# The low halves of eleven weight blocks by an adding transfer: a two-layer decoder trunk in split float32 on one core

## Chip, core and metric

The kernel runs on one core of a Trainium2 chip. The metric is the device time of one execution in microseconds (us); lower is better. Engines are called TensorE (PE, the matrix engine), VectorE (DVE), ScalarE (ACT), GpSimd (POOL) and SyncE (SP, which issues most transfers). L412 is line 412 of the kernel before. Lines of the changed kernel are higher, by 1 from line 46 on and by 7 behind `convert`: L750 is L757 there.

## What is computed

A trunk of two layers on 512 tokens of width 1024. Each layer has one input projection whose columns feed three mixers side by side (RWKV-7, retention and latent attention), an output projection, and a gated feed-forward part. The reference, cut to its frame:

```python
for l in range(DEPTH):                       # DEPTH = 2
    hn = rms_norm(h, attn_norm[l])
    proj = hn @ w_in[l]                      # 512 x 1024 @ 1024 x 2592
    p_a, p_b, p_c = split(proj)              # RWKV 896, retention 1024, latent attention 672 columns
    y_a, v_first = rwkv7_mixer(p_a, ...)     # layer 2 mixes v with layer 1's v_first
    y_b = retention_mixer(p_b, positions)
    y_c = mla_mixer(p_c, positions, ...)     # q and kv latents -> w_q_up, w_kv_up -> causal softmax
    h = h + concat(y_a, y_b, y_c) @ w_out[l]
    hn = rms_norm(h, ffn_norm[l])
    gu = hn @ w_gate_up[l]                   # D_FF = 2816
    h = h + (silu(gu[..., :D_FF]) * gu[..., D_FF:]) @ w_down[l]
return rms_norm(h, final_norm)
```

## The kernel before

**Split products.** Activations lie transposed in SBUF, features on the partitions and the 512 tokens along them. Each float32 operand of the large products is held as two halves of the type float32r: `hi`, the rounded value, and `lo`, what the rounding left. `gemm` makes a product of three matmuls for each piece of 128 rows: hi with hi, hi with lo, lo with hi, 512 columns each (a "group" in what follows). A block of eight such pieces, [8, 128], has 1024 columns in SBUF.

**The weight stream.** All weights pass through in one fixed sequence of blocks, 102 in the first layer, so that layer 2 begins with block 102. SyncE loads a block to one of three buffers `wr` (`fetch`, L395, 512 KB for 1024 columns). `convert` (L405 to L413) makes its halves in two rings of three buffers: ScalarE copies `wr` to `wh`, which rounds it (L411), and then VectorE, or GpSimd for the blocks listed in `POOL_LO`, subtracts: `wl = wr - wh` (L412). `wnext` asks for conversions so that three blocks are ready, and `gemm` reads `wh` twice before it reads `wl`. In layer 2, blocks 113 to 115 are the retention values with the rotary key (`VGROUPS`: 864, 864 and 576 columns; their matmuls have 288 columns), 116 and 117 the retention gate, 118 and 119 the latents of keys and values, 120 to 122 those of the queries, 123 and 124 `w_kv_up`, 125 to 127 `w_q_up` (768 columns each), and 128 the first of `w_out`.

**Order.** The program is written by generators that a `Driver` interleaves: `dense` gives the large products, and `rwkv`, `chain`, `group_norm`, `retnet`, `head` and others give the small steps of the mixers in between. A step yields a due time from the table `T`, in thousands of cycles of the driver's own clock, which counts the matmuls issued so far; the generator with the best priority whose time has come goes on. The table `EN` names the engine of a small operation by a key (`d` VectorE, `p` GpSimd, `a` ScalarE). Each engine then runs its instructions in the order in which they were written, apart from moves that the framework's scheduler makes by its own estimates.

**The steps near the change, in layer 2.** In `rwkv` the value residual is made by a difference, a product (L690, key e564) and a sum (L691, e565); L711 to L715 are exponentials on ScalarE, whose results VectorE multiplies at L720 to L724; L730 and the halves behind it make two more operands; at L746 TensorE makes 16 products of 64x128 for each PSUM pair, and VectorE copies them out under a mask (L750), two copies for each pair. `pm` has four PSUM buffers, so the third pair of products waits for the first copies. In between, `dense` writes the retention queries and keys: VectorE scales a product (L1150), four transfers exchange rows of it (L1152), and L1153 to L1155 rotate it. Later, L821 and L829 move pieces of a triangular inverse from PSUM, `retnet` squares a product (L952) and multiplies with the gate (L959), `group_norm` ends with L887 to L893 (L348 and L349 belong to its inverse root), and `head` makes the softmax: scores in a PSUM buffer of `pd`, a maximum (L984), an exponential (L986).

```python
act.copy(hi[:, z], t[:, z])                                                    # L411
(pool if on in POOL_LO else dve).tensor_tensor(lo[:, z], t[:, z], hi[:, z].bitcast(F32), ALU.subtract)
...
E("e564").tensor_tensor(s, s, vf[:, b, :], ALU.mult)                           # L690
E("e565").tensor_tensor(v_[:, b, :], v_[:, b, :], s, ALU.add)                  # L691
...
dve.tensor_tensor(o, pg[par].rearrange("p (j w t) -> p j w t", j=4, w=2), m, ALU.mult)   # L750
...
dve.tensor_tensor(t, ps, rB, ALU.mult)                                         # L1150
```

Of the kernel before, what the change touches and what calls it, by code (L numbers as in the profile page):

```python
# [15 lines left out]
AF = mybir.ActivationFunctionType  # L16
ALU = mybir.AluOpType
# [115 lines left out]
def lay_out(inp):  # L133
# [57 lines left out]
def tile_trunk(ctx: ExitStack, tc: tile.TileContext, a: dict, out: bass.AP, dbg=None):  # L191
    nc = tc.nc
    act, dve, pool, sp = nc.scalar, nc.vector, nc.gpsimd, nc.sync
# [17 lines left out]
    def E(key):  # L211
        return {"d": Dve, "p": pool, "a": Act}[EN[key]]

    def times(key, o, x, f):

        if EN[key] == "a":
            act.activation(o, x, AF.Identity, scale=f)
        else:
            {"d": dve, "p": pool}[EN[key]].tensor_scalar(o, x, f, None, ALU.mult)

    def nm(s):
        uid[0] += 1
        return f"{s}_{uid[0]}"
# [6 lines left out]
    def r2(shape=(P, S), dt=F32):  # L230
        return mp.tile(list(shape), dt, tag="r2", name=nm("r2"), bufs=NR)
# [4 lines left out]
    def sm(shape, dt=F32, tag="sm", bufs=4):  # L236
        return mp.tile(list(shape), dt, tag=tag, name=nm(tag), bufs=bufs)
# [167 lines left out]
    def convert(at=0):  # L405

        t, i, j, parts, on = raw(at)
        hi, lo = (wp.tile([P, i * j], F32R, tag=n, name=nm(n)) for n in ("wh", "wl"))
        for part in range(parts):
            z = slice(part * i * j // parts, (part + 1) * i * j // parts)  # L410
            act.copy(hi[:, z], t[:, z])  # L411
            (pool if on in POOL_LO else dve).tensor_tensor(lo[:, z], t[:, z], hi[:, z].bitcast(F32), ALU.subtract)  # L412
        stream["ready"].append((1.0, tuple(z.rearrange("p (i j) -> p i j", i=i) for z in (hi, lo))))  # L413

    def load_next(parts=1):
        plan.pop(0)
        fetch(parts)
        convert()
# [14 lines left out]
    def sums(last, down, end, start):  # L433
# [30 lines left out]
        if down and not start:  # L464
            yield convert()
# [67 lines left out]
    def tables():  # L533
        yield T[0]["tables1"]
        posi = r2((P, S), I32)
# [8 lines left out]
        def angles(inv, tok=False):  # L544
# [962 lines left out]
```

## Time and profile before

| | us |
|---|---|
| median of 3 runs | 1308.99 |
| lowest and highest run | 1302.78, 1310.22 |
| the profiled execution | 1300.39 |
| its span in the trace | 1298.6 |

The mean granted clock of TensorE over the span is 0.993 of full speed. The page gives the busy time of each engine, and queries of the trace give the same for any stretch, the waits of an engine with what ended each, and single instructions in order of time. A busy time counts an engine's instructions, not what they wait for; the idle time in brackets behind an instruction is followed by what released it.

### The profile page before, as it was taken

To read this page: it belongs to the slowest core of one execution; us is meant where nothing else is said; L and a number is where in the kernel's file an instruction comes from. 1 tells how busy PE (TensorE), PEld (TensorE's weight loads), DVE (VectorE), ACT (ScalarE), POOL (GpSimd) and SP (SyncE) were. 2 spreads that over 40 slices of the span, in tenths; PEclk is the share of its full clock that TensorE was granted. 3 is DMA by queue.
4 is the path that set the end of the run, shared out by engine and by line. 5 is a ranking of instruction groups with operands and counts; after the bars stand their busy time and mean duration, and the time that the engine had idled before them with its cause. 6 is when DMAs were issued, how large, how long until landed. Compare 5 with 4: busy or idle time off the path is not lost.

```text
span 1298.6 us, 20237 instructions
## 1 busy us (share of the span) xinstructions
PE 1266.0 (97%) x7802; PEld 1089.0 (84%) x7802; DVE 988.0 (76%) x1647; ACT 683.3 (53%) x1273; POOL 114.8 (9%) x101
## 2 busy tenths in 40 slices
PE   7999999999999999999999999989999999999997
PEld 5788788678899999999877887856888999999996
DVE  7797876857987777777668697686679877777774
ACT  7834456835554444445475345465455544444454
POOL 1040112301000000000012300132100000000000
PEclk9999999999999999999999999989999999999999
DMA  7435423123233333333522523140322333222231
GB/s 250 138 92 158 102 70 110 33 66 98 82 114 98 101 111 98 101 95 106 186 91 85 135 85 78 49 164 1 98 97 74 108 113 98 97 98 98 82 114 65
DMA packets 67512, 131.14 MB, mean 101 GB/s; under 512 B 29044, under 2 KB 33940, under 8 KB 67416
## 3 DMA queue, kind: packets, MB, share of 16 engines
q1 hardware_dynamic: 66040, 128.23, 31.7%
q8 instruction: 61, 1.00, 0.3%
q10 hardware_dynamic: 1232, 1.09, 0.3%
q0 software_dynamic: 144, 0.52, 0.1%
q14 instruction: 35, 0.29, 0.1%
HBM read 117.50 MB, written 9.18 MB: 98 GB/s over the span
## 4 chain that ended last, share of the span: by engine, by line
PE 89%; DVE 5%; ACT 3%; DMA 1%; issue 1%; SPq 0%; DVEq 0%; ACTq 0%
PE pd L251 61%; PE pm L251 26%; PE pm L258 2%; DMA wr<-in_wts_dram 1%; DVE wl L412 0%; DVE r L730 0%; DVE r L1469 0%; DMA u<-in_xT_dram 0%; DVE wl L430 0%; DVE u L724 0%; DVE u L1025 0%; DVE u L720 0%; DVE u L1246 0%; ACT wh L411 0%; DVE r L440 0%
## 5 line engine op out<-in xcount | busy, mean ns | idle before, releaser
L251 PE MATMUL pd<-u,wh 128*128 128x256 f32 (+1 forms) x3136 | 757.9, 334 | 9.7 <-ACT wh L411 5.9
L251 PEld LDWEIGHTS pd<-u,wh 128*128 128x128 f32 x3136 | 530.1, 191 | 70.6 <-issue 7.3
L251 PE MATMUL pd<-u,wl 128*128 128x256 f32 (+1 forms) x1568 | 519.7, 331 | 0.2
L251 PEld LDWEIGHTS pd<-u,wl 128*128 128x128 f32 x1568 | 299.4, 191 | 28.6 <-POOL wl L412 0.8
L251 PE MATMUL pm<-u,wh 128*128 128x512 f32 (+1 forms) x800 | 211.9, 352 | 0.0
L411 ACT CAST wh<-wr 128x1024 fp32r<-128x1024 f32 (+3 forms) x102 | 98.8, 974 | 146.3 <-PE pd L251 86.3
L251 PEld LDWEIGHTS pm<-u,wh 128*128 128x128 f32 x800 | 139.1, 190 | 17.9
L251 PE MATMUL pm<-u,wl 128*128 128x512 f32 (+1 forms) x400 | 140.5, 351 | 0.0
L429 ACT CAST wh<-r 128x512 fp32r<-128x512 f32 x144 | 87.4, 618 | 98.6 <-PE pm L251 51.7
L412 DVE TENSOR_TENSOR wl<-wr,wh 128x1024 fp32r<-128x1024 f32 (+4 forms) x86 | 99.1, 1156 | 42.6 <-ACT wh L411 42.4
L429 ACT CAST wh<-wr 128x512 fp32r<-128x512 f32 x108 | 66.9, 620 | 79.5 <-PE pm L251 54.1
L430 DVE TENSOR_TENSOR wl<-r,wh 128x512 fp32r<-128x512 f32 x144 | 97.6, 687 | 8.1 <-ACT wh L429 6.0
L430 DVE TENSOR_TENSOR wl<-wr,wh 128x512 fp32r<-128x512 f32 x108 | 74.3, 689 | 24.1 <-ACT wh L429 21.8
L251 PEld LDWEIGHTS pm<-u,wl 128*128 128x128 f32 x400 | 75.8, 190 | 10.2
L412 POOL TENSOR_TENSOR wl<-wr,wh 128x1024 fp32r<-128x1024 f32 (+4 forms) x16 | 34.8, 2176 | 504.1 <-ACT wh L411 504.1
L1392 DVE TENSOR_TENSOR u<-u,pm 128x512 f32<-128x512 f32 x64 | 43.6, 684 | 43.7 <-PE pm L251 43.7
L251 PE MATMUL pm<-u,u 32*32 32x32 f32 (+4 forms) x728 | 67.4, 277 | 3.8 <-DVE u L750 2.8
L251 PEld LDWEIGHTS pm<-u,u 32*32 32x32 f32 (+3 forms) x728 | 50.5, 157 | 20.7 <-issue 13.6
L411 ACT CAST wh<-gg 128x1024 fp32r<-128x1024 f32 x32 | 33.6, 1049 | 41.7 <-issue 27.7
L440 DVE TENSOR_TENSOR r<-r,wr 128x512 f32<-128x512 f32 x72 | 49.5, 687 | 0.6
L251 PE MATMUL pd<-u,u 96*128 96x512 f32 (+3 forms) x128 | 45.2, 467 | 4.3 <-ACT u L986 3.6
L412 DVE TENSOR_TENSOR wl<-gg,wh 128x1024 fp32r<-128x1024 f32 x32 | 39.1, 1222 | 7.8 <-ACT wh L411 7.8
(272 smaller groups left out, 1593.8 us busy)
## 6 DMA issues: line engine op xcount, KB each, us to landing
wr<-in_wts_dram SPq DMA_DIRECT2D x142, 512.0 KB, 3.5
gg<-in_wts_dram SPq DMA_DIRECT2D x32, 512.0 KB, 3.3
wr<-in_wts_dram SPq DMA_DIRECT2D x22, 384.0 KB, 3.0
u<-in_xT_dram SPq DMA_DIRECT2D x7, 512.0 KB, 6.8
tb<-tab_d SPq DMA_DIRECT2D x8, 256.0 KB, 4.7
r<-r SPq DMA_DIRECT2D x32, 64.0 KB, 2.0
h_d<-u SPq DMA_DIRECT2D x4, 512.0 KB, 2.9
u<-h_d SPq DMA_DIRECT2D x4, 512.0 KB, 7.4
```

The source lines that it names most:

```text
L251: tc.keep_in_program_order(nc.tensor.matmul(o, lhsT, rhs, start=start, stop=stop, skip_group_check=True))
L258: tc.keep_in_program_order(nc.tensor.transpose(o, x, idn))
L411: act.copy(hi[:, z], t[:, z])
L412: (pool if on in POOL_LO else dve).tensor_tensor(lo[:, z], t[:, z], hi[:, z].bitcast(F32), ALU.subtract)
L429: act.copy(hi[:, z], t)
L430: dve.tensor_tensor(lo[:, z], t, hi[:, z].bitcast(F32), ALU.subtract)
L440: E(key).tensor_tensor(o, x, y, ALU.add)
L1392: dve.tensor_tensor(hk(m), hk(m), ps, ALU.add)
```

## The change

For the eleven blocks in the new list `DMA_LO` the conversion is written differently: ScalarE writes the negated rounded weights to `wl`; GpSimd issues a transfer that reads the same weights from DRAM again and adds them onto `wl`; ScalarE makes `wh` as before. VectorE or GpSimd (block 115) subtracts nothing there. `POOL_LO` changes too: in layer 1 blocks 23 and 27 go from GpSimd to VectorE, and 8 and 31 the other way; in layer 2 block 115 becomes a transfer, 129 and 134 go to VectorE, 117, 130 and 140 to GpSimd. In `EN` the product e564 (L690) goes from GpSimd to VectorE and the sum e565 (L691) from VectorE to GpSimd. In `T` 21 due times of layer 1 and 11 of layer 2 are other numbers.

```diff
-POOL_LO = (0, 12, 21, 23, 26, 27, 30, 35, 38, 106, 110, 115, 129, 134, 137)
+DMA_LO = (113, 114, 115, 118, 119, 120, 121, 122, 125, 126, 127)
+POOL_LO = (0, 8, 12, 21, 26, 30, 31, 35, 38, 106, 110, 117, 130, 137, 140)
...
-        stream["raw"].append((t, i, j, parts, stream["next"] - 1))
+        stream["raw"].append((t, src, i, j, parts, stream["next"] - 1))
...
-        t, i, j, parts, on = raw(at)
+        t, src, i, j, parts, on = raw(at)
...
             z = slice(part * i * j // parts, (part + 1) * i * j // parts)
+            if on in DMA_LO:
+
+                act.activation(lo[:, z], t[:, z], AF.Identity, scale=-1.0)
+                pool.dma_start(lo[:, z], src[:, z], accum_op=ALU.add)
+                act.copy(hi[:, z], t[:, z])
+                continue
             act.copy(hi[:, z], t[:, z])
```

The orders of the engines before and after the change follow for three places. In a row, `u`, `r` and `tb` are tiles in SBUF, `pd` and `pm` tiles in PSUM, and the last number of a name counts the tiles.

**VectorE at the masked copies of layer 2 (place A).** Before:

```order
L730 SCALAR_TENSOR_TENSOR r_1331_7122<-u_6882,PC,u_6657 128x512
L412 TENSOR_TENSOR wl_7148<-wr_7145,wh_7147 128x864
L730 SCALAR_TENSOR_TENSOR r_1332_7123<-u_6882,PC,u_6657 128x512
L1150 TENSOR_TENSOR r_1337_7134<-pd_7043,rB_6622 128x512
L1150 TENSOR_TENSOR r_1351_7205<-pd_7144,rB_6622 128x512
L750 TENSOR_TENSOR u_7172<-pm_7176,C 128x8x64
L750 TENSOR_TENSOR u_7172<-pm_7177,C 128x8x64
```

and in the changed kernel:

```order
L737 SCALAR_TENSOR_TENSOR r_1331_7117<-u_6882,PC,u_6657 128x512
L737 SCALAR_TENSOR_TENSOR r_1332_7118<-u_6882,PC,u_6657 128x512
L1157 TENSOR_TENSOR r_1337_7135<-pd_7052,rB_6622 128x512
L757 TENSOR_TENSOR u_7168<-pm_7172,C 128x8x64
L757 TENSOR_TENSOR u_7168<-pm_7173,C 128x8x64
L757 TENSOR_TENSOR u_7169<-pm_7188,C 128x8x64
L757 TENSOR_TENSOR u_7169<-pm_7189,C 128x8x64
L757 TENSOR_TENSOR u_7170<-pm_7204,C 128x8x64
L757 TENSOR_TENSOR u_7170<-pm_7205,C 128x8x64
L1161 TENSOR_TENSOR r_1338_7136<-r_1338_7136,tb_6923 128x512
L1157 TENSOR_TENSOR r_1355_7233<-pd_7145,rB_6622 128x512
```

The subtraction of block 114 between the two L730 (now L737) is gone, as is that of block 113 further up, and the second L1150 (now L1157) stands behind six of the masked copies. On TensorE, `dense`'s groups between the products that feed the copies are now two of 128x512, taken from ahead of the products, where one of 128x512 and one of 128x288 stood: ahead of the third pair of products one group of each kind fewer is issued.

**GpSimd at the same place.** Before:

```order
L725 TENSOR_TENSOR dsc_7019<-r_1310_7020,emid_7018 128x7
L725 TENSOR_TENSOR dsc_7019<-r_1324_7080,emid_7018 128x7
L315 TENSOR_TENSOR r_1334_7126<-r_1331_7122,r_1333_7125 128x512
L315 TENSOR_TENSOR r_1336_7131<-r_1332_7123,r_1335_7130 128x512
L412 TENSOR_TENSOR wl_7224<-wr_7221,wh_7223 128x576
L1153 TENSOR_TENSOR u_7042<-r_1337_7134,tb_6922 128x512
L1153 TENSOR_TENSOR u_7042<-r_1351_7205,tb_6922 128x512
```

and in the changed kernel:

```order
L732 TENSOR_TENSOR dsc_7013<-r_1310_7014,emid_7012 128x7
L415 DMA wl_7056<-in_wts_dram 128x864
L732 TENSOR_TENSOR dsc_7013<-r_1324_7075,emid_7012 128x7
L415 DMA wl_7149<-in_wts_dram 128x864
L316 TENSOR_TENSOR r_1334_7121<-r_1331_7117,r_1333_7120 128x512
L316 TENSOR_TENSOR r_1336_7126<-r_1332_7118,r_1335_7125 128x512
L1160 TENSOR_TENSOR u_7051<-r_1337_7135,tb_6922 128x512
L415 DMA wl_7252<-in_wts_dram 128x576
L1160 TENSOR_TENSOR u_7051<-r_1355_7233,tb_6922 128x512
```

The three transfers of blocks 113 to 115 stand between small operations, and the subtraction of block 115 is gone.

**ScalarE at the first softmax of layer 2 (place C).** Before:

```order
L347 ACTIVATE r_1582_8452<-r_1581_8451 128x512
L888 ACTIVATE r_1571_8414<-r_1571_8414,PC 128x512
L888 ACTIVATE r_1580_8449<-r_1580_8449,PC 128x512
L986 ACT_TABLE_LOAD
L986 ACTIVATE u_8475,ssum_8481<-pd_8477,nmx_8480 128x512
```

and in the changed kernel:

```order
L348 ACTIVATE r_1582_8466<-r_1581_8465 128x512
L895 ACTIVATE r_1571_8428<-r_1571_8428,PC 128x512
L993 ACT_TABLE_LOAD
L993 ACTIVATE u_8486,ssum_8492<-pd_8488,nmx_8491 128x512
L895 ACTIVATE r_1580_8463<-r_1580_8463,PC 128x512
```

The first exponential goes ahead of the second head group's scaling (L888, now L895). On VectorE the first maximum (L984) goes ahead of the second L887 and L889 in the same way. Place B is on ScalarE 60 us earlier, where the copy of the retention output to its rounded half (L305, called from L961) moves from ahead of the two L821 to behind the next square (L951, L952).

## Rows read from the trace of the kernel before

**Rows 1.** The page, part 1: busy us (share of the span) xinstructions of each engine.

```profile
PE 1266.0 (97%) x7802; PEld 1089.0 (84%) x7802; DVE 988.0 (76%) x1647; ACT 683.3 (53%) x1273; POOL 114.8 (9%) x101
```

**Rows 2.** Stretches: length, busy us of PE, PEld, DVE, ACT, POOL; granted clock, DMA share, GB/s.

```profile
17.00:350.00 333.00, 328.27 (x1878) 264.29 (x1879) 261.73 (x484) 193.16 (x365) 57.54 (x46) 0.99 0.33 99
690.00:1000.00 310.00, 298.81 (x1745) 240.37 (x1744) 236.50 (x439) 159.36 (x315) 46.82 (x42) 0.98 0.29 85
155.00:160.00 5.00, 3.29 (x59) 2.56 (x60) 3.42 (x6) 2.99 (x5) 0.00 (x0) 1.00 1.05 221
720.00:730.00 10.00, 8.74 (x64) 7.77 (x65) 9.86 (x14) 1.62 (x3) 9.25 (x11) 0.83 0.46 121
855.00:865.00 10.00, 9.66 (x28) 5.63 (x29) 6.88 (x24) 6.11 (x21) 4.91 (x5) 0.66 0.73 255
```

**Rows 3.** Waits of TensorE from 690 to 1010 us: us, times, longest.

```profile
PE pd L251 <- ACT u L986: 3.6, 1, 3.6
PE pm L251 <- DVE u L750: 2.5, 1, 2.5
PE pm L251 <- ACT r L952: 1.2, 1, 1.2
PE pm L251 <- ACT u L821: 0.8, 2, 0.4
```

**Rows 4.** VectorE's instructions around place A: start us, us, line, operation, [idle before].

```profile
697.38 2.30 DVE L412 TENSOR_TENSOR wl<-wr,wh 128x1024 fp32r<-128x1024 f32 x1
701.30 0.69 DVE L691 TENSOR_TENSOR u<-u,r 128x512 f32<-128x512 f32 x1 [1.62 <-POOL r L690]
...
716.43 1.05 DVE L412 TENSOR_TENSOR wl<-wr,wh 128x864 fp32r<-128x864 f32 x1
717.40 1.78 DVE L730 SCALAR_TENSOR_TENSOR r<-u,PC,u 128x512 f32<-128x512 f32 x1
719.10 1.27 DVE L1150 TENSOR_TENSOR r<-pd,rB 128x512 f32<-128x512 f32 x2
720.30 0.67 DVE L750 TENSOR_TENSOR u<-pm,C 128x512 f32<-128x512 f32 x1
```

**Rows 5.** SyncE's transfers of L1152 at place A.

```profile
696.85 2.46 SPq L1152 DMA_DIRECT2D r<-r  x4
```

**Rows 6.** ScalarE at place B.

```profile
791.30 0.62 ACT L305 CAST u<-r 128x512 fp32r<-128x512 f32 x1 [2.32 <-DVE r L959]
```

**Rows 7.** ScalarE at place C.

```profile
852.38 0.81 ACT L888 ACTIVATE r<-r,PC 128x512 f32<-128x512 f32 x1 [0.51 <-DVE r L887]
```

**Rows 8.** ScalarE's casts of blocks 119, 121 and 127, and TensorE where block 127 starts.

```profile
748.11 1.05 ACT L411 CAST wh<-wr 128x1024 fp32r<-128x1024 f32 x1 [1.95 <-PE pd L251]
...
759.75 1.06 ACT L411 CAST wh<-wr 128x1024 fp32r<-128x1024 f32 x1 [4.10 <-PE pd L251]
...
833.30 0.83 ACT L411 CAST wh<-wr 128x768 fp32r<-128x768 f32 x1 [0.87 <-PE pd L251]
...
843.50 0.62 PE L251 MATMUL pd<-u,wh 128*128 128x512 f32 x2
...
844.19 0.62 PE L251 MATMUL pd<-u,wh 128*128 128x512 f32 x2
```

**Rows 9.** GpSimd's one issue before, and transfers by kind: KB each, us to landing.

```profile
47.29 0.75 POOL L673 DMA_DIRECT2D vf_d<-u  x1 [2.00 <-DVE u L1133]
...
wr<-in_wts_dram SPq DMA_DIRECT2D x142, 512.0 KB, 3.5
wr<-in_wts_dram SPq DMA_DIRECT2D x22, 384.0 KB, 3.0
r<-r SPq DMA_DIRECT2D x32, 64.0 KB, 2.0
u<-h_d SPq DMA_DIRECT2D x4, 512.0 KB, 7.4
vf_d<-u POOLq DMA_DIRECT2D x1, 512.0 KB, 4.2
```

More of the change, by code (lines that the diff above doesn't have):

```diff
@@ L36 @@
 TWO_PI = 2.0 * math.pi
-T = [{'tables1': 0, 'norm1': 0.0, 'p_rwkv': 3.43, 'p_ret': 0, 'p_head': 6.66, 'p_tab': 2.02, 'p_gn': 0.0, 'p_att': 6.0, 'p_kr': 0.0, 'angles1': 0, 'angles2': 3.74, 'angles3': 0.0, 'angles4': 0.46, 'angles5': 3.39, 'rwkv1': 4.34, 'rwkv2': 8.45, 'rwkv3': 0, 'rwkv4': 0.0, 'rwkv5': 0, 'rwkv6': 1.03, 'rwkv7': 0.0, 'rwkv8': 2.74, 'rwkv9': 5.5, 'rwkv10': 3.21, 'rwkv11': 0.76, 'rwkv12': 4.16, 'rwkv13': 2.42, 'rwkv14': 0, 'rwkv15': 0.82, 'rwkv16': 0.36, 'rwkv17': 0.74, 'rwkv18': 14.33, 'rwkv19': 2.06, 'rwkv20': 0, 'rwkv21': 1.12, 'chain1': 0.9, 'chain2': 2.38, 'chain3': 0.55, 'group_norm1': 5.69, 'group_norm2': 3.14, 'group_norm3': 4.58, 'retnet1': 5.58, 'retnet2': 0, 'retnet3': 0.74, 'retnet4': 4.98, 'retnet5': 3.23, 'retnet6': 0, 'head1': 9.39, 'head2': 0.36, 'head3': 4.91, 'head4': 1.99, 'attend1': 1.77, 'key_rope1': 3.62, 'latent_norm1': 6.26, 'latent_norm2': 3.54, 'latent_norm3': 0.33, 'sums1': 2.61, 'sums2': 2.56, 'sums3': 0, 'sums4': 10.27, 'sums5': 3.42, 'sums6': 6.78, 'sums7': 2.65},
-     {'norm1': 0, 'p_rwkv': 5.43, 'p_ret': 7.16, 'p_head': 0, 'p_gn': 2.8, 'p_att': 0, 'p_kr': 5.54, 'rwkv1': 3.33, 'rwkv2': 5.03, 'rwkv3': 0, 'rwkv4': 0, 'rwkv5': 0, 'rwkv6': 3.29, 'rwkv7': 0, 'rwkv8': 7.7, 'rwkv9': 1.93, 'rwkv10': 2.94, 'rwkv11': 0.81, 'rwkv12': 3.89, 'rwkv13': 0.02, 'rwkv14': 0, 'rwkv15': 0.58, 'rwkv16': 0, 'rwkv17': 0.73, 'rwkv18': 13.88, 'rwkv19': 0.0, 'rwkv20': 0.42, 'rwkv21': 0.0, 'chain1': 0.28, 'chain2': 0.96, 'chain3': 0.69, 'group_norm1': 4.53, 'group_norm2': 2.33, 'group_norm3': 19.85, 'retnet1': 2.13, 'retnet2': 4.32, 'retnet3': 0, 'retnet4': 1.4, 'retnet5': 0.0, 'retnet6': 0, 'head1': 5.26, 'head2': 0.0, 'head3': 8.59, 'head4': 0.13, 'attend1': 0.0, 'key_rope1': 1.56, 'latent_norm1': 3.38, 'latent_norm2': 1.41, 'latent_norm3': 0.52, 'sums1': 2.53, 'sums2': 8.37, 'sums3': 7.02, 'sums4': 0.16, 'sums5': 4.5, 'sums6': 5.56, 'sums7': 1.81}]
@@ L41 @@
-EN = {'e499': 'd', 'e535': 'd', 'e541': 'd', 'e542': 'd', 'e563': 'd', 'e564': 'p', 'e565': 'd', 'e592': 'd', 'e593': 'd', 'e594': 'd', 'e595': 'd', 'e757': 'd', 'e759': 'p', 'e773': 'p', 'e826': 'd', 'e968': 'p', 'e969': 'd', 'e970': 'd', 'e909': 'd', 'e1037': 'd', 'e1090': 'd', 'e1096': 'p', 'e1097': 'd', 'e1171': 'd', 'e302': 'd', 'e273': 'd', 'c511': 'a', 'c639': 'a', 'c646': 'a', 'c647': 'a', 'c686': 'a', 'c716': 'a', 'c736': 'a', 'c1008': 'a', 'c498': 'd', 'h1': 'p', 'h2': 'd', 'h3': 'p', 'h4': 'p', 'h5': 'd', 'h6': 'd', 's1': 'd', 's2': 'd', 's3': 'd', 's4': 'd', 'z': 'd', 'x0': 'p', 'x1': 'd', 'x2': 'p', 'x3': 'd'}
+T = [{'tables1': 0, 'norm1': 0.0, 'p_rwkv': 3.43, 'p_ret': 0, 'p_head': 7.87, 'p_tab': 0.0, 'p_gn': 0.0, 'p_att': 5.3, 'p_kr': 0.04, 'angles1': 0, 'angles2': 3.74, 'angles3': 0.0, 'angles4': 5.7, 'angles5': 0, 'rwkv1': 4.34, 'rwkv2': 8.45, 'rwkv3': 0, 'rwkv4': 0, 'rwkv5': 0, 'rwkv6': 1.03, 'rwkv7': 0.0, 'rwkv8': 3.93, 'rwkv9': 2.08, 'rwkv10': 0, 'rwkv11': 0.76, 'rwkv12': 4.16, 'rwkv13': 2.42, 'rwkv14': 0, 'rwkv15': 0.82, 'rwkv16': 0.24, 'rwkv17': 0.74, 'rwkv18': 14.33, 'rwkv19': 2.06, 'rwkv20': 0, 'rwkv21': 0, 'chain1': 0.94, 'chain2': 2.38, 'chain3': 0.55, 'group_norm1': 5.69, 'group_norm2': 3.14, 'group_norm3': 4.75, 'retnet1': 5.58, 'retnet2': 0, 'retnet3': 1.21, 'retnet4': 4.98, 'retnet5': 3.23, 'retnet6': 0, 'head1': 9.39, 'head2': 0.36, 'head3': 4.91, 'head4': 1.99, 'attend1': 1.77, 'key_rope1': 3.62, 'latent_norm1': 6.26, 'latent_norm2': 1.2, 'latent_norm3': 0.33, 'sums1': 0, 'sums2': 0, 'sums3': 0.99, 'sums4': 14.85, 'sums5': 5.48, 'sums6': 4.38, 'sums7': 2.65},
+     {'norm1': 0, 'p_rwkv': 5.43, 'p_ret': 7.94, 'p_head': 0, 'p_gn': 2.8, 'p_att': 0, 'p_kr': 4.9, 'rwkv1': 3.33, 'rwkv2': 4.39, 'rwkv3': 0, 'rwkv4': 0.0, 'rwkv5': 0, 'rwkv6': 3.29, 'rwkv7': 0, 'rwkv8': 7.7, 'rwkv9': 1.45, 'rwkv10': 2.94, 'rwkv11': 0.81, 'rwkv12': 4.08, 'rwkv13': 0.02, 'rwkv14': 0, 'rwkv15': 0.58, 'rwkv16': 0, 'rwkv17': 0.73, 'rwkv18': 13.88, 'rwkv19': 0.0, 'rwkv20': 0.42, 'rwkv21': 0.0, 'chain1': 0.28, 'chain2': 0.96, 'chain3': 0.69, 'group_norm1': 5.32, 'group_norm2': 2.33, 'group_norm3': 15.83, 'retnet1': 2.13, 'retnet2': 4.32, 'retnet3': 0.0, 'retnet4': 1.4, 'retnet5': 0.0, 'retnet6': 0, 'head1': 5.26, 'head2': 0.0, 'head3': 8.59, 'head4': 0.09, 'attend1': 0.0, 'key_rope1': 1.56, 'latent_norm1': 3.38, 'latent_norm2': 1.41, 'latent_norm3': 0.52, 'sums1': 1.71, 'sums2': 8.37, 'sums3': 7.02, 'sums4': 0.16, 'sums5': 3.51, 'sums6': 5.56, 'sums7': 3.62}]
@@ new lines @@
+EN = {'e499': 'd', 'e535': 'd', 'e541': 'd', 'e542': 'd', 'e563': 'd', 'e564': 'd', 'e565': 'p', 'e592': 'd', 'e593': 'd', 'e594': 'd', 'e595': 'd', 'e757': 'd', 'e759': 'p', 'e773': 'p', 'e826': 'd', 'e968': 'p', 'e969': 'd', 'e970': 'd', 'e909': 'd', 'e1037': 'd', 'e1090': 'd', 'e1096': 'p', 'e1097': 'd', 'e1171': 'd', 'e302': 'd', 'e273': 'd', 'c511': 'a', 'c639': 'a', 'c646': 'a', 'c647': 'a', 'c686': 'a', 'c716': 'a', 'c736': 'a', 'c1008': 'a', 'c498': 'd', 'h1': 'p', 'h2': 'd', 'h3': 'p', 'h4': 'p', 'h5': 'd', 'h6': 'd', 's1': 'd', 's2': 'd', 's3': 'd', 's4': 'd', 'z': 'd', 'x0': 'p', 'x1': 'd', 'x2': 'p', 'x3': 'd'}
```

## Prediction

> **What bounds the kernel now.** The page first: TensorE is busy for 97% of the span, VectorE for 76% [rows 1]. The reader should take from this that time can be won only where TensorE pauses or runs at its lower clock; an instruction less on VectorE is worth nothing by itself. The table by stretches comes next [rows 2]. From 690 to 1000 us, the mixing part of layer 2, where all eleven blocks lie, TensorE is busy 298.81 of 310 us, so 11.2 us are open there. The waits of TensorE in that stretch name the pauses [rows 3]: 3.6 us for the softmax (L986), 2.5 us for VectorE's masked copies (L750), 1.2 us for a squared half (L952), 0.8 us for two copies of the triangular inverse (L821). Two of them cost more than their length, because the granted clock falls behind them to the lower of its two levels for a while. In the 10 us around and behind the L750 pause it is 0.83 on the mean, behind the softmax pause 0.66 [rows 2]. Against the full clock these lose 0.17 x 10 = 1.7 us and 0.34 x 10 = 3.4 us. After the pause of 5.00 - 3.29 = 1.71 us in layer 1 the clock stays at 1.00 [rows 2]. Pauses and clock make up everything that layer 2's half of this change can win: about 16 us.
>
> **The pause for L750 (place A).** VectorE is the late one: it goes without a gap from L1150 to L750 and the first L750 starts at 720.30 us [rows 4]. Ahead of that the change removes two subtractions of 864 columns; the shown one holds the engine from 716.43 to 717.40, 0.97 us, and the other is taken at the same. Its place on the other side is covered: the cast of that block no longer stands ahead of ScalarE's exponentials, so VectorE's next operation, which waits for them, can come as much earlier. One of the two L1150 is now issued behind the L750s: half of the step from 719.10 to 720.30, 0.60 us. The swap of the product and the sum (L690, L691) takes away VectorE's wait of 1.62 us for GpSimd. Of this only 0.6 us count, since the operation behind it (L1154, which follows when L691 ends at 702.0) needs transfers that land around 701.3: issued from 696.85 to 699.3 [rows 5], 2.0 us of landing [rows 9]. Sum: 0.97 + 0.97 + 0.60 + 0.60 = 3.1 us. Against it, one group of three 128x512 matmuls and one of three 128x288 fewer stand on TensorE ahead of the product that waits for the first L750. A group of 512 takes 844.19 - 843.50 = 0.69 us [rows 8], one of 288 by its columns 0.39, so TensorE asks 1.1 us earlier. A pause of 2.5 + 1.1 - 3.1 = 0.5 us stays, below the 1.71 us that left the clock alone. Gain: 2.0 us, and the 1.7 us of clock: **3.7 us**. Bounds: 0, if the transfer or a contended row of VectorE eats the margin, and 4.2, if the pause goes whole.
>
> **The small pauses (place B).** ScalarE's cast at 791.30 us stands, waiting for VectorE, ahead of the two L821 copies [rows 6]; it moves behind the next square. The 0.8 us for L821 go; the copies for L829 then find that cast of 0.62 us ahead of them, and I give back 0.3. The 1.2 us for L952 are the latency of ScalarE's own square and stay. Gain: **0.5 us**, bounds 0 and 1.5.
>
> **The softmax pause (place C).** TensorE waits 3.6 us for the first exponential to free a PSUM buffer [rows 3]; this stands behind the second L888 at 852.38 us [rows 7]. In the new order the first maximum (L984) and exponential go ahead of the second head group's L887, L889 and L888. That takes two operations of 0.60 us each (the step of L1150, of the same size) out of VectorE's path, and out of ScalarE's 0.8 us and the wait of 0.5 before it [rows 7]. Against it, the subtraction of block 129, on GpSimd before, now lies on VectorE ahead of L348 (1.05 x 1024/864 = 1.24 us by the row of 864 columns [rows 4]). By the two queues together I get the exponential 1.2 us earlier: **1.2 us**. The pause of 2.4 us that is left is nearer to the 2.5 us at A, which the clock followed, than to 1.71 us, so I leave the 3.4 us as they are. Bounds: 0, and 3.6 + 3.4 = 7.0 us. [...]
>
> **What is added, and what covers it.** ScalarE writes eleven negated copies: five at 1.05 and three at 0.83 us by the casts of the same shapes [rows 8], 864 columns twice at 0.89 and 576 at 0.59 by the columns; together 10.1 us on an engine that is busy 159 of 310 us there [rows 2]; the cover is TensorE's other two blocks in the ring. GpSimd issues eleven transfers. The only one it issues before takes 0.75 us and lands in 4.2 us with 512 KB; a plain load of 512 KB lands in 3.5, one of 384 KB in 3.0 us [rows 9]. The trace has no adding transfer, so it is bounded: 4.2 us if the second reading is hidden; 7.4 + 4.2 = 11.6 us if it pays the slowest load of 512 KB and a whole pass more. I take 4.2 us and the data time of a further 512 KB, 4 x (3.5 - 3.0) = 2.0 us: **6.2 us** (384 KB: 5.2), because the same queue's row is the nearest.
> Against that the room: block 119's cast starts at 748.11 us, when its buffer comes free, and the block is wanted when block 118 ends, at 759.75 us, where block 121's cast starts [rows 8]. From the 11.64 us between go 2 x 1.05 us of ScalarE and 0.75 us of issue: 8.8 us. In front of 121's negated copy stand two more readings of PSUM, 1.3 us, but its period is 1 us longer, so the room is the same. Blocks 113 to 115 have more, since the issue stands behind one small operation or three. Block 127 is the tight one: cast at 833.30, wanted at 843.50 us [rows 8]; from 10.2 us go 0.83 + 0.83 us, about 1.2 us of other ScalarE work in between and the issue, leaving 6.6 us for 5.2. So I cost the transfers at **0**. If they land late, each block waits, and the ring of three buffers passes the delay on. Queued behind the issues on GpSimd are two L905 and the L315 of the group norm; none is near its due time.
> [...]
>
> **Layer 1.** Four subtractions change between VectorE and GpSimd and the due times move some work. TensorE has 333 - 328.27 = 4.7 us of pauses from 17 to 350 us [rows 2], most of them latencies that the change does not touch. I cost this at 0, bounds -0.5 and +1.
>
> **Sum.** 3.7 + 0.5 + 1.2 = 5.4 us. The profiled execution took 1300.39 us for a span of 1298.6; the median of the runs shown is 1308.99, 8.6 us above it, and the lowest run 1302.78. Against the profile the forecast is 1295.0, against the median 1303.6, that is **1304 us**. A measurement of this kernel can tell about 0.5%, 6.5 us, from no change; the forecast lies inside.
>
> **Rivals.**
> 1. The softmax pause shrinks enough for the clock to stay up, or closes. For it: 1.2 us by order, and a VectorE that is 11 us lighter before. Against: it needs a pause nearer 1.7 than 2.4 us. Then 3.7 + 0.5 + 1.2 + 3.4 = 8.8, up to 4.2 + 0.5 + 7.0 = 11.7 us: about **1300 us**, 1297 at best.
> 2. The gain at A is handed back: TensorE, asking 1.1 us earlier, meets VectorE as late as before, or a later step of the same chain (the group of L750 copies, then L759) stalls it and the clock falls there. For it: VectorE is busy 9.86 of the 10 us at A [rows 2]. Then about -1 us: **1308 us**.
> 3. Slower: the adding transfers land late. The point is a landing of about 8.8 us at 512 KB for blocks 118 to 122 and 6.6 us at 384 KB for block 127. At 11.6 us each of five blocks waits about (11.6 - 8.8)/2 = 1.4 us after the first, as three buffers share it, 7 us; block 127 at 9.7 us waits 3, the clock falls once for 1.7 to 3.4 us; less the 5 us won: some 8 us, **1317 us**. For it: an untried kind of transfer. Against: the nearest rows are below half of that.
>
> **How the numbers follow.** Forecast 0.43, rival 1 0.25, rival 2 0.20, rival 3 0.12. Faster by over 0.5%: rival 1 and the part of the forecast's bounds beyond 6.5 us, 0.16, together 0.41. Slower: 0.12. Within: 0.47. The range goes from rival 1's best, 1297, less the 6 us by which the lowest run shown lies below the median, to five above the median, which leaves out the full price of rival 3: 1291 to 1314.
>
> **What would show it.** In the new profile the wait of TensorE for L750 in layer 2 is below 1 us, with the clock at 1.00 in the 10 us behind it; the softmax wait is 2 to 3 us, with a fall behind it; no wait of TensorE ends on one of the eleven transfers; these land in 5 to 8 us; VectorE's busy time falls by about 11 us, ScalarE's rises by 10. The forecast is wrong if TensorE waits for a low half, if the wait for L750 stays above 2 us, or if the clock at the softmax stays up.

## The result and the profile after

| | us |
|---|---|
| the change, median of 9 runs | 1297.58 (1294.82 to 1300.70) |
| before, median of 9 runs | 1303.45 (1301.70 to 1310.22) |
| ratio | 0.9944, 95% interval 0.9930 to 0.9958 |
| the profiled execution of the change, its span | 1298.86, 1297.1 |

Between the medians the change is faster by 5.9 us, 0.45%; by the ratio it is 0.56%, about 7.3 us (5.5 to 9.1). The two profiled executions alone would hide most of it: 1300.39 before is below every other run of before shown, and 1298.86 after is above the median of after. The profiled execution of the repeat further down took 2998.72 us and isn't read; it and two others that took far longer than the rest stand outside the ratios. Lines of the changed kernel are told as in the change: L757 answers to L750, L993 to L986, L419 to L412.

The page of the changed kernel, part 1, and then its table by stretches (length, busy us of the engines, granted clock, DMA share, GB/s):

```profile
PE 1266.6 (98%) x7802; PEld 1088.5 (84%) x7802; DVE 977.1 (75%) x1636; ACT 692.6 (53%) x1284; POOL 126.7 (10%) x112
```

```profile
690.00:1000.00 310.00, 301.46 (x1776) 242.16 (x1775) 234.37 (x439) 169.79 (x329) 58.04 (x53) 0.99 0.39 102
...
670.00:680.00 10.00, 10.00 (x39) 7.20 (x38) 6.17 (x8) 6.89 (x12) 0.37 (x1) 0.70 0.31 107
720.00:730.00 10.00, 9.28 (x81) 7.58 (x81) 8.85 (x15) 3.34 (x6) 8.12 (x8) 1.00 0.70 153
780.00:790.00 10.00, 8.58 (x54) 6.67 (x55) 6.04 (x10) 5.73 (x9) 0.00 (x0) 0.83 0.62 133
855.00:865.00 10.00, 8.72 (x35) 5.49 (x36) 9.56 (x30) 8.22 (x27) 8.15 (x8) 1.00 0.50 167
```

VectorE lost 10.9 us of work against [rows 1], ScalarE gained 9.3. TensorE's open time from 690 to 1000 us shrank from 11.2 [rows 2] to 8.5 us. At place A (720 to 730) the clock is now 1.00, where it was 0.83; behind the softmax (855 to 865) it is 1.00, where it was 0.66. But two falls stand where before had none: 0.70 at 670 us, while TensorE was busy for all of the 10 us, and 0.83 at 780 us. Against the full clock they lose 0.30 x 10 = 3.0 and 0.17 x 10 = 1.7 us in this one execution, whose span is only 1.5 us shorter.

The waits of TensorE from 690 to 1010 us (us, times, longest):

```profile
PE pd L252 <- ACT u L993: 2.6, 2, 2.3
PE pd L252 <- issue: 1.3, 1, 1.3
PE pm L252 <- ACT r L959: 1.2, 1, 1.2
PE pm L252 <- ACT u L836: 1.0, 1, 1.0
PE pm L259 <- DVE u L757: 0.7, 1, 0.7
```

Against [rows 3] the 2.5 us for the masked copies are gone from the products; 0.7 us for them come up at the transposes behind. The softmax wait fell from 3.6 to 2.3 us. No wait ends on one of the eleven transfers. The wait put down to "issue" (nothing that the profile shows) ends at 850.85 us, ahead of the first scores; the same wait of before is shorter:

```profile
PE pd L251 <- issue: 0.7, 1, 0.7
```

VectorE around place A:

```profile
705.24 1.38 DVE L1161 TENSOR_TENSOR r<-r,tb 128x512 f32<-128x512 f32 x1 [0.60 <-DMA r<-r]
...
720.29 0.68 DVE L1157 TENSOR_TENSOR r<-pd,rB 128x512 f32<-128x512 f32 x1
720.90 3.67 DVE L757 TENSOR_TENSOR u<-pm,C 128x512 f32<-128x512 f32 x6
```

One L1157 stands ahead of the six copies, where two L1150 stood in [rows 4]; and further up VectorE waits 0.60 us for the exchange transfer, as worked out for the swap. The adding transfers by size (us from issue to landing):

```profile
wl<-in_wts_dram POOLq DMA_DIRECT2D x5, 512.0 KB, 7.7
wl<-in_wts_dram POOLq DMA_DIRECT2D x3, 384.0 KB, 6.5
...
wl<-in_wts_dram POOLq DMA_DIRECT2D x2, 432.0 KB, 5.7
wl<-in_wts_dram POOLq DMA_DIRECT2D x1, 288.0 KB, 6.6
```

A plain load of 512 KB landed in 3.5 us [rows 9], so the adding one, on another queue, takes 2.2 times as long. An issue on GpSimd takes 0.86 to 0.92 us.

### The profile page after: what moved, and what is told of

Read it like the earlier page. It is cut to its first block, busy times and chain, and to the rows that moved or that the text cites. A ratio compares the mean times of both kernels' runs of the same rounds, so it can differ in the third digit from the quotient of the medians.

```text
span 1297.1 us, 20259 instructions
## 1 busy us (share of the span) xinstructions
PE 1266.6 (98%) x7802; PEld 1088.5 (84%) x7802; DVE 977.1 (75%) x1636; ACT 692.6 (53%) x1284; POOL 126.7 (10%) x112
## 4 chain that ended last, share of the span: by engine, by line
PE 89%; DVE 6%; ACT 3%; DMA 1%; issue 1%; SPq 0%; DVEq 0%; ACTq 0%
PE pd L252 60%; PE pm L252 27%; PE pm L259 2%; DMA u<-in_xT_dram 1%; DVE r L805 0%; DVE wl L419 0%; DVE r L1476 0%; DVE r L737 0%; DVE u L1302 0%; DVE r L806 0%; DVE u L727 0%; DVE u L1032 0%; DVE u L731 0%; ACT L993 0%; DVE r L349 0%
## 5 line engine op out<-in xcount | busy, mean ns | idle before, releaser
L418 ACT CAST wh<-wr 128x1024 fp32r<-128x1024 f32 (+3 forms) x91 | 88.5, 979 | 128.9 <-PE pd L252 66.4
L419 DVE TENSOR_TENSOR wl<-wr,wh 128x1024 fp32r<-128x1024 f32 (+3 forms) x75 | 86.1, 1151 | 32.2 <-ACT wh L418 31.9
L419 POOL TENSOR_TENSOR wl<-wr,wh 128x1024 fp32r<-128x1024 f32 (+2 forms) x16 | 36.5, 2282 | 517.8 <-ACT wh L418 517.8
L252 PEld LDWEIGHTS pm<-u,u 32*32 32x32 f32 (+3 forms) x728 | 50.1, 155 | 17.5 <-issue 10.7
L252 PE MATMUL pd<-u,u 96*128 96x512 f32 (+3 forms) x128 | 42.3, 441 | 4.0 <-ACT u L993 2.6
L419 DVE TENSOR_TENSOR wl<-gg,wh 128x1024 fp32r<-128x1024 f32 x32 | 39.1, 1221 | 7.8 <-ACT wh L418 7.8
```

The costliest lines, as they stand in the source:

```text
L252: tc.keep_in_program_order(nc.tensor.matmul(o, lhsT, rhs, start=start, stop=stop, skip_group_check=True))
```

## The experiments

The theory was that the change wins by what it takes away ahead of two places where VectorE is late, A and C, and that the transfers cost nothing. Its rivals were that the new due times bring the gain (rival 1 of the expectations), or that VectorE's lighter load counts wherever a block lies (their rival 2); the prediction numbers its rivals otherwise. All ratios are to the kernel before, run beside.

**The transfers alone.** The changed code with `T` and `EN` of before (not printed here), and before's GpSimd list without block 115:

```diff
-POOL_LO = (0, 8, 12, 21, 26, 30, 31, 35, 38, 106, 110, 117, 130, 137, 140)
+POOL_LO = (0, 12, 21, 23, 26, 27, 30, 35, 38, 106, 110, 129, 134, 137)
```

> The eleven adding transfers with the due times, the engines of single operations and the GpSimd list of before (block 115 apart). TensorE's order is that of before; VectorE has no subtraction ahead of the first L750 and one L1150 fewer; at the softmax (place C) the order is that of before. Theory (the pause at place A is what the change wins, by what it takes from VectorE ahead of L750): the pause of 2.5 us and its clock loss go, 4.2 us, and place B's 0.5: 4.7 us faster than before, ratio 0.9964; the softmax wait stays at 3.6 us. Rival 1 (the new due times and engines bring the gain, the transfers nothing): 0, ratio 1.000. Rival 2 (VectorE's lighter load counts wherever a block is): the whole 5.9 us, ratio 0.9955.

Measured: 0.9986 (0.9970 to 1.0003), 1302.61 against 1304.54 us: 1.9 us, less than half of what was expected. The pause at the products went, but the copies made TensorE wait 2.4 us at the transposes behind. That wait, and VectorE there:

```profile
PE pm L259 <- DVE u L757: 2.4, 1, 2.4
```

```profile
725.25 0.68 DVE L1157 TENSOR_TENSOR r<-pd,rB 128x512 f32<-128x512 f32 x1
725.85 1.91 DVE L757 TENSOR_TENSOR u<-pm,C 128x512 f32<-128x512 f32 x3
730.82 0.69 DVE L1161 TENSOR_TENSOR r<-r,tb 128x512 f32<-128x512 f32 x1 [3.06 <-DMA r<-r]
731.42 0.68 DVE L757 TENSOR_TENSOR u<-pm,C 128x512 f32<-128x512 f32 x1
```

and SyncE's queue, which issues that exchange:

```profile
727.13 1.36 SPq L759 DMA_DIRECT2D ms_d<-u  x2
728.59 3.17 SPq L1159 DMA_DIRECT2D r<-r  x4
```

The second L1157 ends at 725.93 us, but its exchange is issued from 728.59, behind two transfers of the copies; VectorE stands 3.06 us, and the last copy is queued behind L1161. In the change the first L1161 stands behind six copies, and the wait is 0.7 us. So the transfers need the retuned part beside them; the due times of layer 2 and its GpSimd blocks (117, 130 and 140 in place of 129 and 134) were not tried apart. This is rival 2 of the prediction: a later step of the same chain stalls TensorE.

**No transfer at all.** The change with its blocks subtracted on VectorE (115 on GpSimd):

```diff
-DMA_LO = (113, 114, 115, 118, 119, 120, 121, 122, 125, 126, 127)
+DMA_LO = ()
```

> The changed kernel without a transfer: its blocks are subtracted on VectorE (115 on GpSimd), all else as changed. Theory: at place A VectorE saves only the L1150 and the swap, 1.2 us, while TensorE asks 1.1 us earlier, so a pause of 2.4 us with its clock loss stays; places B and C stand in the order of before: 0 to 0.5 us faster than before, ratio 0.9996 to 1.000. Rival 1 (due times and engines): 5.9 us faster, 0.9955. Rival 2 (VectorE's load): 0, 1.000.

Measured: 1.0023 (1.0007 to 1.0039), 1307.39 us: slower than before by 2.9 us. The retuned part alone brings nothing and costs a little; rival 1 is out. The waits of this kernel at A and C, the softmax wait 1.1 us longer than before:

```profile
PE pd L252 <- ACT u L993: 4.7, 1, 4.7
PE pm L252 <- DVE u L757: 2.6, 1, 2.6
```

**Blocks 113 to 115 alone, and the other eight alone.** Two kernels, each with one part of the list (in the second, block 115 goes to GpSimd as before):

```diff
+DMA_LO = (113, 114, 115)
...
+DMA_LO = (118, 119, 120, 121, 122, 125, 126, 127)
```

> The changed kernel with the transfers of blocks 113, 114 and 115 alone; the other eight are subtracted on VectorE. Place A has the order of the change, places B and C that of before. Theory: 3.7 us faster than before, ratio 0.9972, TensorE's wait for L750 below 1 us, the softmax wait at 3.6 us. Rival 1: 5.9 us, 0.9955. Rival 2: three of eleven parts, 1.6 us, 0.9988.

> The changed kernel with the transfers of blocks 118 to 122 and 125 to 127 alone; 113 and 114 are subtracted on VectorE, 115 on GpSimd. Places B and C have the order of the change, place A keeps both subtractions ahead of L750. Theory: B and C give 0.5 + 1.2 = 1.7 us, ratio 0.9987, up to 5.1 us (0.9961) if the clock stays up behind the softmax pause; the wait for L750 stays at 2 to 2.5 us. Rival 1: 5.9 us, 0.9955. Rival 2: eight of eleven parts, 4.3 us, 0.9967.

Measured: 0.9982 (0.9966 to 0.9999) and 0.9984 (0.9967 to 1.0001), 1302.30 and 1302.31 us. Against the kernel without transfers that is 5.1 us for each part, and their sum of 10.2 us is the whole way from 1307.39 down to the change (in ratios, 0.9944 - 1.0023 = -0.79%). The two parts add up, within intervals of about 0.0016 on each ratio, and each removes its own wait, here of the one and of the other:

```profile
PE pd L252 <- ACT u L993: 4.7, 1, 4.7
...
PE pm L259 <- DVE u L757: 0.7, 1, 0.7
```

```profile
PE pm L252 <- DVE u L757: 2.6, 1, 2.6
...
PE pd L252 <- ACT u L993: 2.5, 1, 2.5
```

Three blocks at A come out worth as much as eight elsewhere, where rival 2 would have given 3/11 and 8/11. The times alone do not exclude that: its 0.9988 and 0.9967 lie inside the first interval and at the edge of the second. What speaks against it is that each part removes its own wait, and the kernel with layer 1's blocks further down.

**Without the latent blocks.** The change with transfers for 113 to 115 and 125 to 127; at C the order is that of the change.

```diff
+DMA_LO = (113, 114, 115, 125, 126, 127)
```

> The changed kernel with the transfers of blocks 113 to 115 and 125 to 127; the five latent blocks 118 to 122 are subtracted on VectorE. Places A and C have the order of the change, place B that of before. The runs before showed the other eight blocks to be worth 0.4% against the same kernel without transfers. Theory now (what counts is the order that the transfers give at A and C, and that the pauses there become too short for the clock to fall): only B's 0.5 us are lost against the change, ratio to before 0.9948, the softmax wait stays below 2.6 us. Rival (VectorE's lighter load counts, block by block): five of eight parts of 5 us are lost, ratio 0.9968, and the softmax wait is above 3 us.

Measured: 0.9970 (0.9953 to 0.9987), 1301.23 against 1305.35 us. The softmax wait is 2.2 us, as the theory has it; the time is that of its rival. The trace has TensorE's waits in layer 2 at 9.4 us in all, against 8.3 with all eleven (8.4 to 9.3 in the two variants below that differ at other places only); the largest new one is 1.1 us for the key rotation (L1194). The rest of the 3.4 us isn't in the waits of the profiled execution, which ran in 1296.91 us, the fastest of 12. The runs differ in the clock: its median over them is 0.991, against 0.994 for the change and 0.992 for its repeat. Whether it is the additional small waits that cost the clock is not shown. So the five latent blocks, which lie at neither A nor C, seem to carry 3.4 us of the gain (by the two intervals, give or take 3), and the theory does not say why; this stays open.

**The swap of L690 and L691 undone.**

```diff
-'e564': 'd', 'e565': 'p'
+'e564': 'p', 'e565': 'd'
```

> The changed kernel with the product L690 on GpSimd and the sum L691 on VectorE again; no other instruction moves. Theory (the swap gives VectorE 0.6 us ahead of the transfer that bounds the next operation, and the pause at L750 has about that much room): 0 to 0.6 us slower than the change, ratio to before 0.9944 to 0.9949, TensorE's wait for L750 below 1 us. Rival (VectorE's whole wait of 1.6 us comes back on the path): a pause of 1 to 2 us at L750 and its clock loss, 1.5 to 3.5 us slower than the change, ratio 0.9956 to 0.9971.

Measured: 0.9941 (0.9922 to 0.9960): the same as the change within 0.2%, and the wait for L757 is 0.7 us again. The swap is worth nothing that shows.

**Every transfer made twice.** To see what a late landing costs:

```diff
-act.activation(lo[:, z], t[:, z], AF.Identity, scale=-1.0)
-pool.dma_start(lo[:, z], src[:, z], accum_op=ALU.add)
+act.activation(lo[:, z], t[:, z], AF.Identity, scale=-2.0)
+for _ in range(2):
+    pool.dma_start(lo[:, z], src[:, z], accum_op=ALU.add)
```

> The changed kernel with each adding transfer made twice, one after the other, onto minus twice the rounded weights, so that the low halves of the eleven blocks come out doubled. The second is issued when the first has landed: a landing of about 7.7 + 0.9 + 7.7 = 16.3 us for 512 KB and 6.5 + 0.9 + 6.5 = 13.9 us for 384 KB. Theory (rooms of 8.8 us for blocks 118 to 122 and 6.6 us for block 127, as predicted): TensorE waits for low halves, about (16.3 - 8.8)/2 = 3.7 us at each of five blocks and 7 us at block 127, with the clock falling behind them: 20 to 35 us slower than the change, ratio to before 1.010 to 1.021. Rival (the room is much larger than worked out, and the transfers could be far slower): below 3 us, ratio under 0.997, and no wait on a low half of more than 1 us.

Measured: 1.0188 (1.0150 to 1.0225), 1331.91 us, by the ratios some 32 us slower than the change, near the upper end of the 20 to 35 us that the rooms gave. TensorE now does wait for low halves:

```profile
PE pd L252 <- DMA wl<-in_wts_dram: 15.4, 5, 5.7
PE pm L259 <- DVE u L758: 4.0, 1, 4.0
PE pm L252 <- POOL r L316: 2.5, 1, 2.5
```

15.4 us in five waits, 6.5 at steps of VectorE and GpSimd for which the change waits 0.7 and 0.6 us, and the clock: 0.982 over the span, against 0.991. So the single transfer's 7.7 us at 512 KB fit into the room, and two of them (7.0 us each in this kernel) do not.

**Layer 1 as before, and the change again.** The first has the old due times of layer 1, the old GpSimd blocks there and the old engines; the second is the change itself.

> The changed kernel with layer 1's due times and GpSimd blocks of before and the swap undone: only layer 2's due times, its GpSimd blocks and the transfers are new. Theory (layer 1's part is nothing): ratio to before 0.993 to 0.996, as the change. Rival (layer 1's new due times carry a part, at most the 1 us of the prediction's bound or more): 0.9955 to 0.997.

> The changed kernel itself, once more. Theory (the same pause lowers the clock in one execution and not in the next): ratio to before 0.993 to 0.996; the softmax wait is 2.2 to 2.6 us as before, and the clock loss in the profile, place by place, is another than in the first profile (which had none behind the softmax). Rival (the clock follows from the length of the pause alone): the same falls at the same places, none behind the softmax.

Measured: 0.9939 (0.9921 to 0.9957) and 0.9929 (0.9901 to 0.9957). Layer 1's part of the change is worth nothing that shows within 0.2%. The second expectation's half on the clock is answered by the other kernels with the same order at C, in the next section.

**The blocks of layer 1 by transfers too.** `DMA_LO` with 11 to 13, 16 to 20 and 23 to 25 added (block 12 leaves `POOL_LO`).

> The changed kernel with the same eleven blocks of layer 1 (11 to 13, 16 to 20, 23 to 25) made by adding transfers as well. Theory (TensorE's pauses in layer 1 are latencies, 1.7 us for L341 among them, and not VectorE's backlog): 0 within 2 us of the change, ratio to before 0.993 to 0.996. Rival (VectorE's lighter load counts wherever it is): another 5 us, ratio 0.9906.

Measured: 0.9982 (0.9967 to 0.9997), 1303.00 us: 5 us slower than the change, where the theory had 0 and the rival a gain. VectorE is 14 us lighter from 17 to 350 us, and nothing is won by it, which speaks for the theory; but one block comes late in layer 1:

```profile
PE pd L252 <- DMA wl<-in_wts_dram: 2.3, 1, 2.3
PE pd L252 <- DVE u L341: 1.7, 1, 1.7
```

The clock is at 0.83 in the 10 us around the late block, 1.7 us, so this block costs 2.3 + 1.7 = 4.0 us. The other row, the wait for L341, is 1.7 us in the change too: VectorE's 14 us less did not shorten it. So a transfer in layer 1 had a price, where it landed later than its block was wanted; the rooms there were not worked out.

**Two more blocks ahead of the softmax.** Blocks 128 and 129 added to the list, to shorten the softmax wait further.

> The changed kernel with blocks 128 and 129 made by adding transfers as well: VectorE, which is busy without a gap from 845 us to the first maximum of the softmax, loses two subtractions of 1.2 us there, and the order of the softmax stays. Theory (VectorE's queue sets the exponential, and a pause below 1.7 us leaves the clock up): the softmax wait falls from 2.3 to about 1.0 us, no fall of the clock behind it, 1.3 us and about 2 us of clock on the mean of the runs: ratio to before 0.991 to 0.9935. Rival (the chain behind the group norm is one of latencies, or the two transfers land late): the wait stays at 2 us or more, 0.9944 or slower.

Measured: 0.9991 (0.9973 to 1.0009), 1304.32 against 1305.53 us: 6 us of the gain are lost. The waits of this kernel:

```profile
PE pd L252 <- DMA u<-ro_d: 6.7, 1, 6.7
PE pd L252 <- ACT u L993: 2.3, 2, 1.9
```

The softmax wait shrank only to 1.9 us, and a new wait stands ahead of it: the rotated queries go through DRAM (`ro_d`), and the scores need them. The write of `ro_d`, by the list of transfers of this kernel and of the change:

```profile
ro_d<-r SPq DMA_DIRECT2D x4, 256.0 KB, 8.6
```

```profile
ro_d<-r SPq DMA_DIRECT2D x4, 256.0 KB, 5.0
```

It lands 3.6 us later beside two more adding transfers; the share of the DMA engines is 0.93 from 840 to 845 us, against 0.77 in the change. Whether the bytes or the changed order on SyncE's queue weigh more there is open.

**The narrow products apart.** The fall at 670 us in the change stands behind 24 matmuls of few rows. By the trace of the change, 18 of them use 32 rows (12 of 256 columns and 6 of 512) and six, of 512 columns, use 64, where the expectation has 32 rows for all. This kernel puts full groups between them, by the due times of layer 2 as shown and in layer 1 by the first two.

```diff
-'rwkv3': 0, 'rwkv4': 0.0, 'rwkv6': 3.29
+'rwkv3': 0.4, 'rwkv4': 0.4, 'rwkv6': 0.5
```

> The changed kernel with other due times around the low-rank products of both layers: 24 matmuls that use 32 rows (12 of 256 and 12 of 512 columns), which followed one another for some 4.5 us without a pause, now have a group of three full matmuls after every product but the first of them; the rest of TensorE's order is as changed. In the profiles so far the clock fell right behind this stretch in 9 of 12 executions in layer 1 and in 4 of 12 in layer 2, with TensorE busy throughout. Theory (the narrow products, not a pause, let the clock fall): the clock stays at 1.00 from 40 to 60 us and from 665 to 690 us, and 0.5 to 2 us are won on the change on the mean, ratio to before 0.9920 to 0.9940. Rival (the falls there have nothing to do with these products): a fall of 1.7 us or more at one of the two places, ratio as the change, 0.993 to 0.9945.

Measured: 1.0095 (1.0067 to 1.0123), 1316.52 against 1306.12 us: 1.5% slower than the change, where the theory had a gain. The clock was at 1.00 at both places:

```profile
40.00:60.00 20.00, 18.84 (x77) 12.48 (x75) 11.58 (x15) 13.23 (x21) 5.76 (x3) 1.00 0.48 156
660.00:690.00 30.00, 30.00 (x131) 23.10 (x130) 15.06 (x21) 16.79 (x23) 4.32 (x2) 1.00 0.38 116
```

This one execution does not prove the theory of the clock, since two of the twelve profiles before it (the other eight alone, every transfer twice) had 1.00 at both places as well. And in layer 1 the steps behind came late (3.7 us for L863, 3.1 for L731, and 3.0 for L341, where 1.7 stood), and the clock fell behind them (0.84 at 80 us, 0.83 at 160, 0.72 at 180). The same for layer 2 alone was not tried. No kernel tried beats the change.

## Why the prediction was right, step by step

**The time.** 1304 against a median of 1308.99 was a gain of 5.0, by the sum 5.4 us; 5.9 us were measured between the medians, 7.3 by the ratio, and 1297.58 lies inside the range. The level is lower mostly because before's own median fell to 1303.45 with more runs: the level was missed by about as much as the change is worth. That the sum comes near is in part luck, since the terms below went wrong on both sides.

**Place A: 3.7 us forecast.** Measured in the two profiles: the pause of 2.5 us became 0.7 at the transposes, 1.8 us, and the clock loss of 1.7 us is gone: 3.5 us. The mechanism is the one forecast: counted from the first of the 16 products, the first copy started 5.40 us later before (720.30 [rows 4]) and 2.93 us later in the change (720.90), so 2.5 us were won on them, where the forecast had 3.1 - 1.1 = 2.0. The first products:

```profile
714.90 1.16 PE L251 MATMUL pm<-u,u 64*128 64x128 f32 x16
```

```profile
717.97 1.16 PE L252 MATMUL pm<-u,u 64*128 64x128 f32 x16
```

The terms inside were not all right: the swap's 0.6 us showed nothing when undone. And the 1.7 us of clock are those of one execution: in the two kernels that keep a pause of 2.6 us there (no transfer at all, the other eight alone) the clock is 0.66 from 720 to 730 us, a loss of 3.4 us.

**Place B: 0.5.** The 0.8 us for the two copies are gone, the wait behind them (L829, now L836) rose from 0.6 to 1.0 us (given back: 0.4, forecast 0.3), and the 1.2 us for the square stayed: 0.4 us. Before:

```profile
PE pm L251 <- ACT u L829: 0.6, 1, 0.6
```

**Place C: 1.2, with the clock left as it was.** The softmax wait fell by 1.3 us, but 0.3 came back at the next head and 0.6 ahead of the scores (0.7 to 1.3 us, see the transfers below), so 0.4 us are left in these two executions. The clock is the step that failed: "I leave the 3.4 us as they are". In the change's profile it stayed up, which the prediction had named as a sign of being wrong. For before and six kernels with the order of the change at C (those that wait for `ro_d` there or make every transfer twice are left out), the loss from 843 to 878 us, (1 - granted clock) x 35 us, was:

| kernel | softmax wait, us | granted clock | loss, us |
|---|---|---|---|
| before | 3.6 | 0.90 | 3.5 |
| the change | 2.3 | 1.00 | 0 |
| layer 1 as before | 2.4 | 0.95 | 1.75 |
| swap undone | 2.4 | 0.95 | 1.75 |
| without the latent blocks | 2.2 | 0.90 | 3.5 |
| the other eight alone | 2.5 | 0.85 | 5.25 |
| layer 1 by transfers too | 2.8 | 0.90 | 3.5 |

Two of its lines, before and the change:

```profile
843.00:878.00 35.00, 30.67 (x135) 20.97 (x134) 29.64 (x65) 23.70 (x54) 13.37 (x11) 0.90 0.47 157
```

```profile
843.00:878.00 35.00, 30.68 (x144) 20.73 (x144) 33.30 (x74) 24.84 (x59) 13.13 (x12) 1.00 0.50 164
```

A pause of 2.2 to 2.5 us took anything from nothing to 5.25 us; for waits of 2.2 to 2.4 us alone it was 0, 1.75 and 3.5 us. So the clock at C should have stood in the sum as a mean, not as an all or nothing. How large the difference of the means is stays open: the three kernels nearest to the change (the change, layer 1 as before, swap undone) lost 1.2 us on the mean, all six with its order at C 2.6, and before's 3.5 are one execution.

**Where the gain sits.** How it divides between pauses and clock is not settled. Over the runs beside each other, before had a median clock of 0.989 and the variant with layer 1 as before 0.992: 0.003 x 1306 = 3.9 us of its 6.8 us would be clock if every loss of clock cost its full length, which the last section shows it doesn't. Runs at the same clock point to less: at 0.988, four runs of before took 1304.45 to 1308.46 us and three of the variant 1299.79 to 1301.94, 5.7 us less by their medians. In the traces all rows of TensorE's waits from 690 to 1010 us, those not shown too, add up to 10.7 us before and 8.3 after, 2.4 less, so part of the gain stands in no wait that the profile shows. The forecast's 3.7 us of pauses and 1.7 of clock are neither borne out nor refuted.

**The transfers: 0.** Right for the low halves: no wait ends on them. Not quite right for other traffic: the write of the rotated queries, which took 4.2 us to land in layer 2 before, takes 5.0 in the change (shown above):

```profile
ro_d<-r SPq DMA_DIRECT2D x4, 256.0 KB, 4.2
```

By the lists of transfers (medians over the writes of both layers) it took 4.8 us with layer 1 as before, 4.9 with every transfer made twice and 5.1 without the latent blocks, all three with transfers for blocks 125 to 127; but 3.2 with layer 1's blocks by transfers too. In the change the second of these writes is issued at 843.65 us; with 5.0 us for it and 2.1 us for reading it back the queries are there at 850.75, and TensorE's "issue" wait of 1.3 us ends at 850.85. Before, 842.53 + 4.2 + 2.1 gives 848.83, and the wait of 0.7 us ends at 848.96. So by these two executions the transfers cost about 0.6 us there, a term that the prediction put at nothing; with layer 1's blocks by transfers too the wait is 0.7 us again. The landing of 6.2 us was mis-sized, 7.7 for 512 KB (and 6.5 for 5.2 at 384 KB); it stayed below the rooms, 8.8 and 6.6 us, with little to spare for the second. That the rooms have an end is shown by the doubled transfers. With two blocks more, that same small transfer on another queue became the bound. GpSimd's issue took 0.86 to 0.92 us, against 0.75 before.

**Layer 1: 0.** Right within 0.2%, by the kernel with layer 1 as before.

**The rivals.** Rival 1 (the clock stays up at C) holds for part of the executions. Rival 2 is what the transfers do without the due times. Rival 3 needed a landing of 8.8 us at 512 KB, and 7.7 were measured; with every transfer made twice it came true.

## What to carry to other kernels

Where one engine is busy for 97% of the time, ask what each pause costs with the clock behind it, and take that clock as a mean over executions: two kernels whose waits differ by 2.4 us differed by 5.9. Subtractions moved from VectorE to transfers paid here at a place where TensorE waits for VectorE (three blocks at A, 5.1 us); in layer 1 they paid nothing, though the five latent blocks seem to have paid 3.4 us, of which the traces explain about 1. Give every added transfer a room of its own (8.8 and 6.6 us here by the prediction's estimate, for landings of 7.7 and 6.5), and look at the small transfers beside it that others wait for: the write of the rotated queries landed in 4.2 us before, in 5.0 in the change and in 8.6 with two blocks more. When a change consists of a mechanism and of retuned times, run each alone: here the one gave 0.14%, the other lost 0.23%, and both together won 0.56%.

## What had not been expected of the hardware

**The clock fell without a pause.** At 670 us of the changed kernel TensorE runs the 24 matmuls of 32 and 64 rows in a row; its instructions there (the row of 10 is told by its first; six of the ten have 64 rows):

```profile
670.85 1.33 PE L252 MATMUL pm<-LR,r 32*128 32x256 f32 x9
...
672.48 3.54 PE L252 MATMUL pm<-r,LR 32*128 32x512 f32 x10
675.95 1.22 PE L252 MATMUL pd<-u,wh 128*128 128x512 f32 x2
...
681.04 0.62 PE L252 MATMUL pd<-u,wh 128*128 128x512 f32 x2
```

Two full matmuls take 1.22 us right behind them and 0.62 five microseconds later. The granted clock is 0.99 from 673 to 674 us, 0.50 from 674 to 680 and 1.00 from 681 on (1.00 and 0.50 are the two levels that the traces of before and of the change show), so here it fell while the last narrow matmuls still ran. TensorE was busy for all of the 10 us from 670 to 680. Of the first 12 profiles, the clock fell at the end of the same stretch or right behind it in 7 in layer 1 (in two more behind the 1.6 us wait that follows it there; the expectation above counts these with them) and in 4 in layer 2, and in neither place in the kernel that put full groups in between. As that is one execution, and two of the 12 had no fall in either place too, that the narrow matmuls are the cause is likely but not shown.

**A wait can absorb what the clock lost.** In layer 1 the stretch is followed by a wait for ScalarE (L659, L652 before). Where the clock stayed up until then (the other eight alone) this wait is 1.6 us; where it fell right behind the stretch it is 0.2 us (before) or 0.3 us (layer 1 as before), with a loss of 1.7 us in these 10 us. So 1.6 - 0.2 = 1.4 of the 1.7 us are taken up by the wait, and the fall costs some 0.3 us. The wait in the other eight alone, and before:

```profile
PE pm L252 <- ACT r L659: 1.6, 1, 1.6
```

```profile
PE pm L251 <- ACT r L652: 0.2, 1, 0.2
```
